# An emission planner's TensorE clock: a constant is added to each product's modelled time

## The chip, the cores and the metric

The program runs on one core of a Trainium2 chip. The time is that of the whole program on the device, in microseconds (us), taken as the median of several runs; less is better. A profiled execution gives the trace of every instruction. Engines are named as the profile does: PE is TensorE (PEld its weight loads), DVE is VectorE, ACT is ScalarE, POOL is GpSimd, SP is the sync engine, which issues the weight DMAs.

## What is computed

Two transformer blocks over 256 tokens of 1024 features, in float32. Cut to what matters:

```python
def reference(x, p, ...):
    x = first_block(x, p, ...)          # layer 0 and layer 1
    return second_block(x, p_2, ...)    # the third layer

def first_block(x, p, ...):
    for i in range(2):
        h = rms_norm(x, g[0])
        m = neighborhood_attention(h, ...) if i == 0 else diff_attention(h, ...)
        x = x + rms_norm(m, g[1])
        x = x + rms_norm(conv_glu_ffn(rms_norm(x, g[2]), ...), g[3])   # width 2816
        x = x + sigmoid(rms_norm(x, g[4]) @ ple_w_gate[i]) * (p[i] @ ple_w_proj[i])
    return x

def second_block(x, p, ...):
    h = x + 0.5 * swiglu(...)                       # width 2816
    u = rms_norm(h) @ w_in                          # the mixer
    o_hg = rms_norm(hgrn2_chunkwise(...)) * silu(hg)    # gated linear recurrence, 4 heads
    o_mla = causal_block_attention(...)             # latent attention, 4 heads
    h = h + concat([o_hg, o_mla]) @ w_out
    h = h + 0.5 * swiglu(...)
    h = h + sigmoid(rms_norm(h) @ w_ple_gate) * (p @ w_ple_proj)
    return rms_norm(h)
```

## The kernel before

Weights arrive in pieces of 128 x 1024 numbers, in the order in which they are used: SP issues the DMA into `raw` (5 buffers), ACT copies it to `hi` (rounded to the type fp32r), DVE subtracts the two into `lo` (9 buffers of each). Activations are split in the same manner (`xh` and `xl`, or a pair of `gx`). A float32 product is then three fp32r products on PE, high by high, high by low and low by high (`mm3`). Streams of such products are nearly all that PE does: with 256 columns where the result is feature-major (`s_chunk`), with 512 where it is token-major (`MStage`, which works on the two halves of 128 tokens apart).

Between these products stand short groups of plain fp32 products: scores of the attentions (`qk`), transposes of probabilities (`cst,e`), probabilities by values (`v,pts`), turns of a head's output (`flip,on`), transposes of the normed input of the next stage (`cst,xs`), and the steps of the recurrence (`qp,kp`, then `hvt,at` and `hvt,qr`, then transposes `cst,hgt` of the normed output). In the recurrence the heads go in two groups of two pairs; a group is done in one PSUM bank `pss`.

Each engine carries out its instructions in the order of its queue. That order is fixed as the program is built. A small model, `Model`, keeps a clock for each engine while the program is emitted: `Engine.call` passes an instruction on (which is why all of the profile's rows show one line, L237) and moves the clocks by the duration that `Engine.cost` gives. `MStage` and `s_chunk` emit the products one by one and call `q()` after each: this emits every other step whose operands are ready by the model's PE clock (plus H = 0.6 us), and calls `fill(t)`, which emits the `hi` or `lo` of a later weight where the model has ACT or DVE idle at that time. `get` and `get_any` choose among the PSUM banks in the same way. So a modelled duration sets where an instruction stands in its queue, and nothing else; on the chip it takes the time that it takes. `take()` emits a weight's parts at the latest before the product that needs them.

The line of the change, in `Engine.cost`, gives a product's duration from its columns n:

```python
            n = free(ins[1])
            dur = n / 2400 * (2 if name == "transpose" else 1 if ins[1].dtype == F32R and n >= 256 else 4)
```

Of the kernel before, what the change touches and what calls it, by code (L numbers as in the profile page):

```python
# [28 lines left out]

# columns of the packed per-feature vectors  # L30
COLS = {}
# [13 lines left out]
NCOL = _col_layout()  # L45
# columns of the shape-only constants
C_ID, C_CM, C_FX, C_NA, C_LV = 0, 128, 384, 385, 385 + 384
# [46 lines left out]
def _spairs(wa, wb):  # L94
    """Chunks of one 128-column block of wa and the same one of wb."""
    k, n = wa.shape
    w = np.stack([wa, wb]).reshape(2, k // 128, 128, n // 128, 128)
    return w.transpose(3, 2, 0, 1, 4).reshape(n // 128, 128, -1)
# [61 lines left out]
class Model:  # L160
    """Engine clocks in us as the program is emitted: they only choose the order of emission."""

# [64 lines left out]
class Engine:  # L227
    """Passes instructions on and keeps the model's clocks."""

# [20 lines left out]
    def cost(self, name, outs, ins, func):  # L250
        free = lambda ap: math.prod(ap.shape[1:])
        n = max(free(ap) for ap in outs + ins)
        ps = any(ap.space == PSUM for ap in outs + ins)
        if name == "dma_start":
            size = outs[0].shape[0] * n * 4 / 330e3
            return 1.04 if self.k == "POOL" else 0.06, [o for o in outs if o.space == SBUF], ins, size
        if self.k == "PE":
            n = free(ins[1])
            dur = n / 2400 * (2 if name == "transpose" else 1 if ins[1].dtype == F32R and n >= 256 else 4)
        elif self.k == "ACT":  # L260
            small = sum(1 for ap in ins if free(ap) == 1 and n > 1) + (len(outs) > 1)
            dur = ((61 if ps else 112) + n) / 1200 + 0.093 * small
            s = self.m.SETS.get(func)
            if s and s != self.m.set:
                self.m.set = s
                dur += 1.28
        elif self.k == "DVE":
            rate = 1.0
            if name == "reciprocal":
                rate = 7.0  # L270
            elif name == "tensor_tensor_scan":
                rate = 1.0
            elif name in ("tensor_scalar", "tensor_copy") and not ps:
                rate = 0.5
            scalar = name in ("tensor_scalar", "scalar_tensor_tensor") and any(
                free(ap) == 1 and ap.space == SBUF for ap in ins[1:]
            )
            dur = (66 + n * rate) / 960 + 0.061 * scalar
        else:
            dur = dict(tensor_tensor=0.3 + 0.164 * n, tensor_scalar=0.262).get(name, 0.02 + n * 0.85e-3)  # L280
        return dur, outs, ins
# [3 lines left out]
def body(ctx: ExitStack, tc: tile.TileContext, A: dict, out: bass.AP, dbg=None):  # L285
# [37 lines left out]
    def get(*tags):  # L323
        """In a step: waits for banks and for the operands of a product."""
        at = cur[0][1] + TO_PE - SP
        while True:
            free = [sorted(banks[t])[tags.count(t) - 1:] for t in tags]
            if all(free):
                at = max([at] + [f[0] + TO_PE - SP for f in free])
                if at <= M.now + 1e-6:  # L330
                    return [claim(t) for t in tags]
                yield (at,)
            else:
                yield (M.now + 0.3,)

    def get_any(*tags):
        """In a step: waits for a bank of any of these kinds."""
        at = cur[0][1] + TO_PE - SP
# [11 lines left out]
    def get_now(*tags):  # L350
        """In the products: waits for banks."""
        until(lambda: all(len(banks[t]) >= tags.count(t) for t in tags))
        return [claim(t) for t in tags]

    def put(*tags):
        """The last reader has been emitted."""
        for t in tags:
            banks[t].append(M.fin)

    def slot(n, shape, dt=F32, name="g"):  # L360
        """One of the 4 KB slots that the stages share."""
        return M.tile(big, 1, shape, dt, f"g{n}", name)
# [14 lines left out]

    # ---- the order of emission: products in quanta; everything else in steps between them, each
    # when the model has its operands ready ----
    fg, cur = [], [None]  # L380
# [49 lines left out]

# [1 line left out]
    subs = []  # L432
# [38 lines left out]
    def fill(t):  # L471
        """Parts of later weights, on engines that the model has idle."""
        while not W["hold"]:
            i = W["next"]
            if lows and M.clk["DVE"] <= t:
                prep_lo()
            elif i in raws and raws[i][1] <= t and i - W["freed"] < NS and len(lows) < 2 and M.clk["ACT"] <= t:
                prep()
            else:
                return  # L480
# [12 lines left out]

# [1 line left out]
    def split(hi, lo, src):  # L495
# [7 lines left out]
    def mm3(o, s, m, first, last):  # L503
        """o += s.T @ m for operands in (hi, lo) parts."""
        pe.matmul(o, s[0], m[0], start=first, stop=False)
# [6 lines left out]
    class Rows(list):  # L512
        """Feature-major operand; a half of it is ready once its writers are emitted."""

# [7 lines left out]
    class MStage:  # L522
        """Token-major acc[half][column block] = lhs.T @ W, contraction outermost."""

# [80 lines left out]
    def s_chunk(p, xt):  # L605
        """p[:, 256 b : 256 b + 256] = (W block b).T @ xt, for a pair of blocks."""
        for b in range(2):
# [8 lines left out]

# [1 line left out]
    def rstd(ss, n, dim):  # L618
# [6 lines left out]
    def rstd2(ss):  # L625
        """From two partial mean squares."""
        ms = sm.tile([128, 1], F32, tag="ms2", name="ms2")
# [30 lines left out]
    def norm_T(h, ss, gi, xt, pair=None, slow=True):  # L658
        """xt[:, half h] = (x rows * rstd * gain).T"""
        rs = rstd2(ss)  # L660
# [48 lines left out]
    def epi_post(h, acc, ok, gp, gi, xt, pair=None):  # L709
        """x += rms_norm(acc) * gp, then the next norm's transposed rows."""  # L710
        ss = sm.tile([128, 2], F32, tag="ss", name="ss")
# [27 lines left out]
    def epi_add(h, acc, ok, scale, gi, xt, pair=None):  # L739
        """x += scale * acc, then the next norm's transposed rows."""  # L740
        ss = sm.tile([128, 2], F32, tag="ss", name="ss")
# [11 lines left out]
    def epi_gate(h, acc, ok, pp, after, warm=False):  # L753
        """x += sigmoid(acc) * pp."""
        cut = [(0, 512), (512, 768), (768, 1024)] if len(acc) == 3 else [(0, 512), (512, 1024)]
# [32 lines left out]

# [1 line left out]
    def ffn_in(i, xt):  # L790
# [32 lines left out]

# [1 line left out]
    def ple_load(i, free=lambda: True):  # L825
        """The transposed embedding in parts, ahead of its product."""
        pt = w2([128, 512], "pt")
# [46 lines left out]

# [1 line left out]
    def na_bias(bm):  # L876
# [120 lines left out]

# [1 line left out]
    def t5_table():  # L999
# [109 lines left out]

# [1 line left out]
    def rope_tables():  # L1111
# [25 lines left out]
    def lower_bound():  # L1137
        """Columns: lb (4 heads), 1 - lb (4 heads)."""
        c0 = COLS["lb"]
# [23 lines left out]
    def mixer(xt):  # L1163
# [20 lines left out]
        ready = [None] * 8  # L1184
        # latent queries and keys, token-major; recurrent gates
        cq = slot(13, [128, 2, 448], name="cq")
# [57 lines left out]
        for h in range(2):  # L1244
            for m in (mc, mg):
                for c in range(4):
                    m.mm(c, h)
        # recurrent queries and gates, feature-major
        def gates(hd):
# [13 lines left out]
        for hd in range(HB):  # L1263
            gates(hd)
        # up-projections
        until(lambda: st["ct"] is not None)
# [43 lines left out]

    def hgrn(g, HQ, KP, QP, FT, TT, HV, HG, AT, ATC, AX_, masks, ready, st):
        """Two heads' scores by doubling: spans of length n meet over QP = q * (decay from the span's start) and
        KP = k * (decay to the span's end); every factor is a product of gates."""
        hs, cs_ = slice(2 * g, 2 * g + 2), slice(4 * g, 4 * g + 4)
# [21 lines left out]
        n = 1  # L1336
        while n < 128:
# [8 lines left out]
            else:  # L1346
                act.activation(at[0:64, :, 64:128], bank[0:64, 0:256].rearrange("p (a t) -> p a t", a=4), AF.Copy)
            # spans of length 2 n
            nb = 512 // (2 * n)
# [105 lines left out]

# [1 line left out]
    for nm in ("na", "da"):  # L1457
# [43 lines left out]
    def first(xt):  # L1501
        """Both halves of the first norm, together with the first weights."""
        ss = [sm.tile([128, 2], F32, tag="ss", name="ss") for _ in range(2)]
# [121 lines left out]
```

## Time and profile before

| | |
|---|---|
| median of 3 runs | 1234.1 us (1233.93 to 1235.17) |
| the profiled execution, its span | 1236.9 us (an execution of its own: no other time of it is listed) |
| PE busy | 1210.5 us of the span, 98% |
| DVE busy, ACT busy | 793.3 us, 702.3 us |
| mean granted clock of PE | 0.991 |
| DMA | 214.52 MB, 173 GB/s on average |

How to read it: PE is at work nearly all of the time, so what a change can win or lose lies in the stretches where PE waits, and in those after them where its granted clock is at the lower of its two levels. The span is 2.8 us over the median; a difference in us that is read from the trace is carried over to the median as it is.

### The profile page before, as it was taken

How to read it: one execution, taken by the hardware profiler on the slowest of the kernel's cores; microseconds unless marked ns; L12 is line 12 of the kernel's file. 1: busy time of each engine (PE TensorE's matmuls, PEld its weight loads, DVE VectorE, ACT ScalarE, POOL GpSimd, SP SyncE). 2: the span in 40 equal slices, each digit the busy share in tenths (PEclk: the TensorE clock that was granted, in tenths of full speed). 3: DMA queues.
4: the chain of work that ended last, by engine and by line, in shares of the span. 5: the costliest groups of instructions: out<-in, count | busy, mean ns of one | idle time of the engine just before them, and what ended most of it. 6: DMA issues, size and time to landing. Idle time of an engine off the chain costs nothing.

```text
span 1236.9 us, 21626 instructions
## 1 busy us (share of the span) xinstructions
PE 1210.5 (98%) x8550; PEld 1097.7 (89%) x8550; DVE 793.3 (64%) x1461; ACT 702.3 (57%) x1273; POOL 50.0 (4%) x89
## 2 busy tenths in 40 slices
PE   8999999999989998999999999999999999999997
PEld 6998899998869877999988799998898789999886
DVE  6866776664666876886645765554566676555445
ACT  6556865553766566765545754443565576444344
POOL 0000100000100212000000000000000010000001
PEclk8999999999999998999999999999999999999999
DMA  8835365565265224575563276555443266555630
GB/s 277 255 136 196 123 226 188 186 204 192 99 221 188 85 92 143 181 257 194 186 209 135 90 267 204 186 179 194 137 162 121 78 204 226 184 186 182 210 121 34
DMA packets 61798, 214.52 MB, mean 173 GB/s; under 512 B 7001, under 2 KB 9817, under 8 KB 61697
## 3 DMA queue, kind: packets, MB, share of 16 engines
q1 hardware_dynamic: 61696, 213.15, 51.6%
q8 instruction: 67, 1.10, 0.4%
q14 instruction: 35, 0.28, 0.1%
HBM read 211.01 MB, written 1.06 MB: 171 GB/s over the span
## 4 chain that ended last, share of the span: by engine, by line
PE 75%; issue 18%; DVE 2%; ACT 2%; POOL 1%; DMA 1%; POOLq 0%; ACTq 0%
PE psa L237 39%; PE pss L237 18%; PE pst L237 18%; POOL rs L237 1%; DVE lo L237 1%; POOL ms L237 1%; ACT junk L237 0%; DMA raw<-in_fi 0%; DMA x<-in_x 0%; ACT xh L237 0%; DVE x L237 0%; DVE xl L237 0%; ACT e L237 0%; DVE e L237 0%; DVE sct L237 0%
## 5 line engine op out<-in xcount | busy, mean ns | idle before, releaser
L237 DVE TENSOR_TENSOR lo<-raw,hi 128x1024 fp32r<-128x1024 f32 (+1 forms) x390 | 471.8, 1216 | 196.8 <-ACT hi L237 195.0
L237 ACT ACTIVATE hi<-raw 128x1024 fp32r<-128x1024 f32 (+1 forms) x390 | 405.9, 1051 | 241.1 <-PE psa L237 103.2
L237 PE MATMUL psa<-hi,gx 128*128 128x512 f32 (+1 forms) x1088 | 344.4, 391 | 2.6 <-ACT gx L237 2.3
L237 PEld LDWEIGHTS psa<-hi,gx 128*128 128x128 f32 x1088 | 204.5, 189 | 45.7 <-ACT gx L237 3.4
L237 PE MATMUL psa<-lo,gx 128*128 128x512 f32 (+1 forms) x544 | 211.2, 388 | 1.5 <-DVE lo L237 1.4
L237 PE MATMUL pst<-xh,hi 128*128 128x256 f32 x704 | 199.2, 283 | 0.0
L237 PE MATMUL pst<-xl,hi 128*128 128x256 f32 x704 | 199.2, 283 | 0.0
L237 PE MATMUL pst<-xh,lo 128*128 128x256 f32 x704 | 199.2, 283 | 0.0
L237 PE MATMUL pss<-xh,hi 128*128 128x256 f32 x672 | 190.5, 283 | 0.7 <-DVE xl L237 0.6
L237 PE MATMUL pss<-xl,hi 128*128 128x256 f32 x672 | 190.3, 283 | 0.0
L237 PE MATMUL pss<-xh,lo 128*128 128x256 f32 x672 | 190.2, 283 | 0.0
L237 PEld LDWEIGHTS pst<-xh,hi 128*128 128x128 f32 x704 | 135.2, 192 | 0.0
L237 PEld LDWEIGHTS pst<-xl,hi 128*128 128x128 f32 x704 | 135.2, 192 | 0.0
L237 PEld LDWEIGHTS pst<-xh,lo 128*128 128x128 f32 x704 | 135.2, 192 | 0.0
L237 PEld LDWEIGHTS pss<-xh,hi 128*128 128x128 f32 x672 | 129.0, 192 | 2.2 <-DVE xl L237 1.0
L237 PEld LDWEIGHTS pss<-xl,hi 128*128 128x128 f32 x672 | 129.0, 192 | 0.2 <-DVE xl L237 0.2
L237 PEld LDWEIGHTS pss<-xh,lo 128*128 128x128 f32 x672 | 129.0, 192 | 0.0
L237 PEld LDWEIGHTS psa<-lo,gx 128*128 128x128 f32 x544 | 102.7, 189 | 21.6 <-DVE lo L237 2.3
L237 PE MATMUL psa<-xh,hi 128*128 128x256 f32 x352 | 105.6, 300 | 1.0 <-ACT xh L237 1.0
L237 PE MATMUL psa<-xl,hi 128*128 128x256 f32 x352 | 100.7, 286 | 0.3
L237 PE MATMUL psa<-xh,lo 128*128 128x256 f32 x352 | 100.1, 284 | 0.0
L237 PEld LDWEIGHTS psa<-xh,hi 128*128 128x128 f32 x352 | 67.6, 192 | 6.8 <-issue 4.7
(239 smaller groups left out, 1441.4 us busy)
## 6 DMA issues: line engine op xcount, KB each, us to landing
raw<-in_fi SPq DMA_DIRECT2D x176, 512.0 KB, 4.6
raw<-in_fo SPq DMA_DIRECT2D x88, 512.0 KB, 3.8
raw<-in_pg SPq DMA_DIRECT2D x24, 512.0 KB, 4.1
raw<-in_na_qk SPq DMA_DIRECT2D x16, 512.0 KB, 5.2
raw<-in_da_qk SPq DMA_DIRECT2D x16, 512.0 KB, 5.6
raw<-in_na_v SPq DMA_DIRECT2D x8, 512.0 KB, 7.5
raw<-in_na_o SPq DMA_DIRECT2D x8, 512.0 KB, 3.6
raw<-in_da_v SPq DMA_DIRECT2D x8, 512.0 KB, 3.7
```

The costliest lines, as they stand in the source:

```text
L237: r = f(*a, **kw)
```

## The change

The duration of a product in the model gets a constant: 13.3 ns for one with fp32r operands, 2.5 ns for any other. An fp32r product of 256 columns goes from 0.1067 us to 0.1200 us, one of 512 from 0.2133 us to 0.2267 us. (An fp32r operand of fewer than 256 columns, which cost four times its columns before, now counts as 256.) The other lines of the diff only take out comments and are left out here.

```diff
         if self.k == "PE":
             n = free(ins[1])
-            dur = n / 2400 * (2 if name == "transpose" else 1 if ins[1].dtype == F32R and n >= 256 else 4)
+            if ins[1].dtype == F32R:
+                dur = max(n, 256) / 2400 + 0.0133
+            else:
+                dur = n / 2400 * (2 if name == "transpose" else 4) + 0.0025
```

The program has the same instructions after it, in another order. Three places:

**V of layer 1, on DVE.** `lo<-raw` is the low part of a weight piece; the pieces of V are, in order of use, raw_3823, then raw_3849 (before) or raw_3846 (after), then raw_3884. `sg`, `x` and `xs` belong to the last norm of layer 0's end, for the second half of the tokens, and `xl` is the split of its transposed result. Before:

```order
L237 TENSOR_TENSOR sg_4013<-sg_4013,pp_1631 128x512
L237 TENSOR_TENSOR x_86<-x_86,sg_4013 128x512
L237 TENSOR_TENSOR lo_3949<-raw_3823,hi_3948 128x1024
L237 TENSOR_SCALAR xs_4067<-x_86,rs2_4064 128x512
L237 TENSOR_TENSOR lo_3969<-raw_3849,hi_3968 128x1024
L237 SCALAR_TENSOR_TENSOR xl0_3748<-pss_4086,cols_88,xh0_3747 128x128
```

After:

```order
L237 TENSOR_TENSOR lo_3944<-raw_3823,hi_3943 128x1024
...
L237 TENSOR_TENSOR sg_4019<-sg_4019,pp_1631 128x512
L237 TENSOR_TENSOR x_86<-x_86,sg_4019 128x512
L237 TENSOR_TENSOR lo_3952<-raw_3846,hi_3951 128x1024
L237 TENSOR_SCALAR xs_4073<-x_86,rs2_4070 128x512
L237 TENSOR_TENSOR lo_3975<-raw_3884,hi_3974 128x1024
L237 SCALAR_TENSOR_TENSOR xl0_3776<-pss_4092,cols_88,xh0_3775 128x128
```

The low part of raw_3823 stood behind the second `x` and now stands twelve rows ahead of it (the rows left out are the eight `xl` of the first half, an `sg` and an `x`); each later one has moved up by one place, so that the one of raw_3884, which came behind the eight `xl` of this half, now stands ahead of them.

**The last two heads of layer 1's attention, on PE.** `v0, v1` by `pts` is the product of a head's values by its probabilities, into `pst`; it is normed, and `flip` turns the normed `on`. Before, pst_5503 is followed (the rows left out are six and three products of 512 columns):

```order
L237 MATMUL pst_5503<-v0_4037,pts_5506 128x128
L237 MATMUL pst_5503<-v1_4038,pts_5506 128x128
L237 MATMUL pst_5454<-flip_94,on_5508 128x128
...
L237 MATMUL pst_5546<-cst_87,e1_5403 128x128 x2
...
L237 MATMUL pst_5546<-v0_4037,pts_5549 128x128
L237 MATMUL pst_5546<-v1_4038,pts_5549 128x128
L237 MATMUL pst_5503<-flip_94,on_5551 128x128
L237 MATMUL psa_5261<-hi_5497,gx_4258 128x512
```

After, pst_5535:

```order
L237 MATMUL pst_5535<-v0_4045,pts_5538 128x128
L237 MATMUL pst_5535<-v1_4046,pts_5538 128x128
L237 MATMUL pst_5557<-cst_87,e1_5432 128x128 x2
L237 MATMUL psa_5282<-hi_5369,gx_4261 128x512
L237 MATMUL psa_5282<-lo_5370,gx_4261 128x512
L237 MATMUL psa_5282<-hi_5369,gx_4261 128x512
L237 MATMUL pst_5557<-v0_4045,pts_5560 128x128
L237 MATMUL pst_5557<-v1_4046,pts_5560 128x128
L237 MATMUL pst_5535<-flip_94,on_5583 128x128
L237 MATMUL psa_5281<-hi_5379,gx_4261 128x512
```

Between a head's `v,pts` and its `flip` stood nine products of 512 columns, another head's `flip`, transposes and values; now three products stand there, with the other head's transposes and values.

**The end of the recurrence in the last mixer, on PE and DVE.** `hvt` by `at` and `qr` ends the second group; `cst,hgt` transposes its normed output. On PE before (30 products of 512 columns stand between, all but one left out, and the first group's transposes):

```order
L237 MATMUL pss_10962<-hvt_10090,at_10096 128x128 x2
L237 MATMUL pss_10962<-hvt_10090,qr_10093 128x128
...
L237 MATMUL pss_10520<-cst_87,hgt_10091 128x128 x4
...
L237 MATMUL psa_11281<-hi_11285,gx_10756 128x512
L237 MATMUL pss_10962<-cst_87,hgt_10091 128x128 x4
L237 MATMUL psa_11239<-hi_11309,gx_11308 128x512
```

After (15 such products stand between, all but one left out):

```order
L237 MATMUL pss_11083<-hvt_10090,at_10096 128x128 x2
L237 MATMUL pss_11083<-hvt_10090,qr_10093 128x128
...
L237 MATMUL psa_11204<-hi_11160,gx_11276 128x512
L237 MATMUL pss_11083<-cst_87,hgt_10091 128x128 x4
L237 MATMUL psa_11203<-hi_11228,gx_11448 128x512
```

On DVE, `ms` is the mean square, from which POOL makes `rs`, and `hgt` is the norming. Before:

```order
L237 SCALAR_TENSOR_TENSOR gx_11308<-pss_10520,cols_88,gx_11308 128x256 x2
L237 TENSOR_SCALAR ms_11344<-ss4_11315 128x4
L237 TENSOR_TENSOR lo_11355<-raw_11111,hi_11354 128x1024
L237 SCALAR_TENSOR_TENSOR hgt_10091<-pss_10962,rs_11345,hgt_10091 128x128 x4
L237 TENSOR_TENSOR lo_11367<-raw_11192,hi_11366 128x1024
```

After:

```order
L237 TENSOR_TENSOR lo_11384<-raw_11244,hi_11383 128x1024
L237 TENSOR_TENSOR lo_11414<-raw_11344,hi_11413 128x1024
L237 TENSOR_SCALAR ms_11419<-ss4_11389 128x4
L237 TENSOR_TENSOR lo_11430<-raw_11366,hi_11429 128x1024
L237 SCALAR_TENSOR_TENSOR hgt_10091<-pss_11083,rs_11420,hgt_10091 128x128 x4
```

The second group has been moved later in the program (a latent attention's scores take its bank first), while the products that use its result stay where they were: fewer products lie between `hvt` and the transposes, and on DVE the `lo` ahead of `ms` is now one of which ACT makes the `hi` behind the sums of squares that `ms` reads.

## Rows read from the trace of the kernel before

**Rows 1.** The page: the span, and the busy time of each engine.

```profile
span 1236.9 us, 21626 instructions
...
PE 1210.5 (98%) x8550; PEld 1097.7 (89%) x8550; DVE 793.3 (64%) x1461; ACT 702.3 (57%) x1273; POOL 50.0 (4%) x89
```

**Rows 2.** Busy time and granted clock of one stretch, by windows (columns: us; PE, PEld, DVE, ACT, POOL busy; PEclk; DMA share; GB/s).

```profile
358.00:361.00 3.00, 3.00 (x8) 2.33 (x8) 3.00 (x4) 0.86 (x1) 0.00 (x0) 0.50 0.72 213
```

**Rows 3.** Timeline of TensorE, 60 us (columns: start, us, engine, line, operation, tiles, shapes, count).

```profile
60.48 0.36 PE L237 MATMUL psa<-xh,hi 128*128 128x256 f32 x1
60.68 0.28 PE L237 MATMUL psa<-xl,hi 128*128 128x256 f32 x1
60.80 0.28 PE L237 MATMUL psa<-xh,lo 128*128 128x256 f32 x1
```

**Rows 4.** Timeline of TensorE, layer 1, products that make V.

```profile
347.25 0.39 PE L237 MATMUL psa<-hi,xh 128*128 128x512 f32 x1
...
349.29 0.39 PE L237 MATMUL psa<-hi,xh 128*128 128x512 f32 x1
350.07 0.50 PE L237 MATMUL psa<-lo,xh 128*128 128x512 f32 x1 [0.39 <-DVE lo L237]
...
352.54 0.50 PE L237 MATMUL psa<-lo,xh 128*128 128x512 f32 x1 [0.81 <-DVE lo L237]
...
353.11 0.27 PE L237 MATMUL pss<-cst,xs 128*128 128x128 f32 x1
...
354.69 0.40 PE L237 MATMUL psa<-hi,xh 128*128 128x512 f32 x1
357.60 0.75 PE L237 MATMUL psa<-lo,xh 128*128 128x512 f32 x1 [2.51 <-DVE lo L237]
...
361.13 0.39 PE L237 MATMUL psa<-hi,xh 128*128 128x512 f32 x1
```

**Rows 5.** Timeline of DVE in the same stretch.

```profile
351.27 1.22 DVE L237 TENSOR_TENSOR lo<-raw,hi 128x1024 fp32r<-128x1024 f32 x1
...
356.33 5.76 DVE L237 TENSOR_TENSOR lo<-raw,hi 128x1024 fp32r<-128x1024 f32 x5
```

**Rows 6.** Timeline of TensorE, end of layer 1's attention.

```profile
450.74 0.50 PE L237 MATMUL psa<-lo,gx 128*128 128x512 f32 x1 [1.37 <-DVE lo L237]
...
463.56 0.60 PE L237 MATMUL pst<-v,pts 128*128 128x128 f32 x4
...
467.25 0.49 PE L237 MATMUL pst<-flip,on 128*128 128x128 f32 x2
...
473.31 0.50 PE L237 MATMUL psa<-hi,gx 128*128 128x512 f32 x1 [1.86 <-ACT gx L237]
...
477.29 0.39 PE L237 MATMUL psa<-lo,gx 128*128 128x512 f32 x1
```

**Rows 7.** Timeline of POOL in that stretch.

```profile
453.95 0.55 POOL L237 TENSOR_TENSOR rs<-ms,nhalf 128x1 f32<-128x1 f32 x1 [6.19 <-DVE ms L237]
...
465.41 1.40 POOL L237 TENSOR_TENSOR rs<-ms,nhalf 128x1 f32<-128x1 f32 x1 [2.31 <-DVE ms L237]
```

**Rows 8.** Timeline of TensorE, end of the last mixer.

```profile
989.67 0.60 PE L237 MATMUL pss<-hvt,at 128*128 128x128 f32 x4
...
998.32 0.60 PE L237 MATMUL pss<-cst,hgt 128*128 128x128 f32 x4
```

**Rows 9.** Timeline of ACT there.

```profile
992.19 0.22 ACT L237 ACTIVATION_READ_ACCUMULATOR junk<-pss 128x1 f32 x1
...
993.74 3.90 ACT L237 ACTIVATE hi<-raw 128x1024 fp32r<-128x1024 f32 x4
998.95 0.48 ACT L237 ACTIVATE gx<-pss,cols 128x256 fp32r<-128x256 f32 x1 [1.31 <-PE pss L237]
```

**Rows 10.** Timeline of DVE there.

```profile
994.28 0.16 DVE L237 TENSOR_SCALAR ms<-ss 128x4 f32<-128x4 f32 x1
...
995.97 1.12 DVE L237 SCALAR_TENSOR_TENSOR hgt<-pss,rs,hgt 128x128 f32<-128x128 f32 x4
```

## The prediction, written before the kernel was run

> **What bounds the kernel now.** The page comes first: PE is busy for 1210.5 of 1236.9 us [rows 1]. The weights, the splits and the steps between products are on engines that are busy for 793 us at most, so the products' own time is a floor that an order can't move; what is open is the waiting between them and the clock behind a wait.
>
> The timeline of PE then gives the price of a product that waits for nothing. Two fp32r products of 256 columns start 0.12 us apart (60.68 to 60.80) [rows 3]. Ten of 512 columns start from 347.25 to 349.29, nine steps of 0.2267 us [rows 4]. Less columns by 2.4 GHz (0.1067 and 0.2133), both leave 0.0133 us. The model of before is short by that for every product, so its PE clock runs ahead of the chip's own pace; the changed one agrees with these rows. This says only that the planner's clock is truer, not that its order is better: it emits a step where the model has its operands ready plus H, and what was late on the chip may have been so by other durations (ACT, DVE, POOL, DMA), which stay as they were.
>
> The third view is the timeline around PE's waits, to see who came last. Three places matter.
>
> *V of layer 1.* PE waits for a `lo` of DVE three times: 0.39 us at 350.07, 0.81 at 352.54, 2.51 at 357.60 [rows 4]. From start to start, less 0.227, they cost 0.55 (349.29 to 350.07), 0.98 (the idle 0.81 and 0.17 of emptying the array, as at the other two) and 2.68 us (354.69 to 357.60). Behind the last one the granted clock is 0.50, the lower of the two levels, 1.2 GHz [rows 2], and eight products take 3.53 us to 361.13, where 1.82 would do: 1.71 us more. In all 5.9 us.
>
> *End of layer 1's attention.* 1.37 us for a `lo` at 450.74, and 1.86 us for `gx` at 473.31; behind the second the ten products to 477.29 take 3.98 us where 2.27 would do, 1.71 us more [rows 6]. In all 4.9 us.
>
> *End of the recurrence.* Nothing is lost there before: from `hvt` at 989.67 to the transposes at 998.32 PE has products to do [rows 8].
>
> **The change part by part.** The instructions are the same, so only places in queues are costed. Each sum is made in the profiled execution, whose span is 2.8 us above the median; I carry the difference over to 1234.1 us.
>
> *V of layer 1.* Each `lo` is one place earlier in DVE's queue: that of the piece which PE waited for at 350.07 is made long before, and the one made in its place serves the next piece. The `lo` that ended the wait at 352.54 started at 351.27 [rows 5]; it now serves a piece that PE wants only six products (1.36 us) later. So the first two waits go (1.53 us), and PE comes to the transposes of `xs` at 351.6 and not at 353.11. What is late next is the first `lo` behind the eight `xl`. Before, from the transposes to the product that had waited for such a `lo` it took 4.49 us (353.11 to 357.60) [rows 4, 5], and PE had 1.81 us of work in between. After, it has six products more: 4.49 - 1.81 - 1.36 = 1.3 us of waiting, and I add 0.3 for transposes that may meet `xs` before it is made. With no drop of the clock behind so short a wait: 5.9 - 1.6 = 4.3 us won. With a drop 2.6; with neither the 0.3 nor a drop 4.6.
>
> *End of layer 1's attention.* The parts of the weights are emitted well ahead, so the 1.37 us go. The last `gx` now has six products ahead of its use and fewer `hi` ahead of it on ACT, so the 1.86 us go. But between the values of a head (`v,pts`) and its `flip` nine products have become three. Before, the pair took 3.69 us from 463.56 to 467.25, hardly waiting [rows 6]: sums of squares on ACT, `ms`, `rs` on POOL, `on` on DVE. The work that PE now has in that time is about 1.75 us (three products 0.68, the other head's transposes and values 0.7, the switches). That gives 1.9 us of waiting; two `lo` now stand ahead of `ms`, so up to 2.8; I take 2.2. POOL's `rs` is part of that chain: it took 0.55 us at 453.95 and 1.40 at 465.41 [rows 7], and I count the long one, since a `lo` stands behind `ms` here too. By the Trainium skill (SBUF — State Buffer, section on the two separate sides) DVE and POOL share a port pair, which the one that is first holds for its whole instruction, so that POOL waits out a `lo`; by the short `rs` the wait would be 0.85 us less and the total by as much lower. By that rule the long one is right, and the two durations agree with it. Net 2.7 us won (4.9 - 2.2); if the clock drops behind the new wait, 1.0; at the long end of the wait with a drop, 0.4; at the short end without, 3.0 and, with the short `rs`, 3.8.
>
> *End of the recurrence.* The transposes of the second group come 15 products behind `hvt` and not 30. Let `hvt` start at T. Before, the sums of squares ended at 992.41, T + 2.7 [rows 8, 9]. Behind them ACT now makes the `hi` (0.98 us, four in 3.90 [rows 9]) whose `lo` (1.22 [rows 5]) DVE has ahead of `ms`: `ms` starts at T + 5.0. From `ms` to `hgt` it took 1.69 us (994.28 to 995.97) and `hgt` 1.12 [rows 10], so `hgt` is done at T + 7.8, and the transposes start at T + 8.0. PE gets there at T + 1.26 (the group itself) + 15 x 0.227 + 0.1 = T + 4.8: 3.2 us of waiting where there was none. Then the next product wants `gx`: ACT started it 0.63 us after the transposes, for 0.48 us [rows 8, 9], against 0.36 us of transposes: 0.8 us more. Together 4.0. Queued behind the waiting transposes are all the products of the output projection, and nothing else can go on PE. If ACT had that `hi` made before the sums of squares, it would be 2.3 us less. The wait is longer than the 2.51 us that were followed by the lower clock, so I add 1.7: 5.7 us lost; bounds 1.7 and 6.
>
> *Groups of fp32 products between fp32r ones.* By the order there are nine more of them (120 before, 129 after), since steps are no longer emitted in one batch. Behind such a group the first step is 0.20 us where 0.12 is due (60.48 to 60.68) [rows 3], 0.08 more; ahead of it I take as much. Nine by 0.16 is 1.4, by three times 0.08 is 2.2; I take 1.7 us lost.
>
> *The feed-forward parts and the rest.* There `hi` and `lo` are made tens of products ahead before and after, and PE waits for none of them: nothing, give or take 1 us for small waits that come or go.
>
> Sum: -4.3 - 2.7 + 5.7 + 1.7 = +0.4 us. Within the halves of this sum that I trust least (whether the clock drops) that is no change: 1234.4 us.
>
> **The rivals.**
>
> *The gains stay and the losses don't come (faster).* If ACT's `hi` is made in time, the wait at the recurrence is 1.7 us and no drop follows it, and the sum is -4.3 - 2.7 + 1.7 + 1.7 = -3.6, 1230.5 us; with the short `rs` 1229.6. For it: the parts of the weights are emitted earlier nearly everywhere in the order, so ACT may be less pressed. Against it: ACT's queue has the `hi` behind the sums.
>
> *Both new waits drop the clock (slower).* At the attention's end the new wait (2.2) is nearer to the 1.86 us that were followed by the lower clock than to any that wasn't [rows 6]. Then its gain is 1.0 and the sum +2.1; with the wait at its long end (0.6 more) and V's shorter gain of 2.6 (1.7 more) it is +4.4: 1236.2 to 1238.5 us. It decides from a wait of about 2 us at the `flip` on.
>
> *The order changes and the time doesn't.* PE is fed in all the long stretches, and if V's waits only move to the pieces behind (its gain 2.6 at least) while recurrence and attention give their losses back, the sum stays within 1 us: this lies with my forecast. By the Trainium skill (TensorE: Matmul & The Clock Gate, on the back-to-back gap) an isolated product takes its columns and 2.5 ns, so that the new constant would be 10.8 ns too long and the planner late to the other side; the 13.3 ns of the rows at 60.68 and 347.25 speak against that, and I give it nothing.
>
> **How the numbers follow.** Less than 0.2%, 2.5 us, can't be told from no change here. The forecast with its own range of 1231.7 to 1236.5 has 0.38; the faster rival, with what may be won beyond it by small waits, 0.32, down to 1227 us; the slower one, with new small waits, 0.30, up to 1241. To leave out no more than 2 in 10, one of each side: 1228.5 to 1239.5 us. Faster 0.32, same 0.38, slower 0.30.
>
> **What would show it.** In the profile after: V of layer 1 with one wait for `lo` of 1 to 1.6 us, near 353 to 356, and full clock behind it; the end of layer 1's attention with a wait of 2 us for `on` ahead of a `flip`, and none for `lo`; near 990 to 1000 a wait of 3 us for `hgt` ahead of `cst,hgt`, with products at the lower clock behind it. Wrong would be: V with its 2.5 us wait still there (the planner's places then don't decide it, a DMA or POOL does); no wait at the recurrence (the `hi` came earlier than the queue says); or new waits in the feed-forward parts, where I expect none.

## The result, and the profile after

The changed kernel takes 1250.8 us (median of 4 runs, 1247.16 to 1252.3) against 1234.63 us before (4 runs): the ratio is 1.0115, with a 95% interval of 1.0094 to 1.0137. The ratio goes by the means, 1250.3 against 1236.0: it is slower by 14 us (the medians differ by 16), and outside the range that was given. The profiled execution has a span of 1248.9 us against 1236.9 [rows 1], a time of its own of 1250.92 us, and a mean granted clock of 0.987 against 0.991. In the executions whose time and span are both listed the span is some 2 us below the time, so the one profiled before, with 1236.9, took about 1239 us, some 3 us over the mean; that is why the two profiles lie only 12.0 us apart.

All 7326 fp32r products stand in the same order in both, so the start of the same product in both traces tells where the time went (us; products numbered from 0; the differences are computed from the two timelines of PE):

```text
product   before    after     difference   what lies between this row and the one above
26        20.02     19.72     -0.30        start
562       120.20    124.29    +4.09        layer 0: attention and its output projection
653       140.00    145.82    +5.82        handover to layer 0's feed-forward part
1914      320.00    325.83    +5.83        feed-forward part
1991      340.01    346.89    +6.88        its end and the gate
2047      360.29    363.04    +2.75        V of layer 1
2602      480.04    482.48    +2.44        layer 1: rest of the attention
2710      500.05    504.46    +4.41        handover to layer 1's feed-forward part
3869      660.17    664.58    +4.41        feed-forward part
4167      720.09    725.50    +5.41        gate, handover to the third layer
5820      1000.15   1005.24   +5.09        feed-forward part, mixer but for its end
5899      1020.05   1031.20   +11.15       end of the mixer, handover
7318      1228.02   1239.17   +11.15       feed-forward part, gate
```

V of layer 1 wins 4.1 us and the end of the mixer loses 6.1, both as forecast. What was not forecast is 4.4 us in layer 0's attention, 1.7 and 2.0 us at the two handovers, 1.0 us at each of the two gates, and that the rest of layer 1's attention wins next to nothing (0.3).

PE's waits by what ended them, the longest groups (columns: what waited, for what; us in total, times, the longest):

```profile
PE pss L237 <- DVE xs L237: 7.2, 5, 1.9
PE pss L237 <- DVE hgt L237: 3.3, 1, 3.3
PE psa L237 <- ACT xh L237: 2.8, 2, 1.4
PE pss L237 <- ACT qk L237: 2.1, 3, 0.9
PE psa L237 <- ACT gx L237: 2.1, 4, 0.6
...
PE psa L237 <- DVE lo L237: 1.3, 1, 1.3
PE pst L237 <- DVE ms L237: 1.3, 1, 1.3
PE psa L237 <- ACT qk L237: 1.2, 1, 1.2
```

In layer 1's V one wait is left of three, 1.35 us idle at 363.04 (from start to start, less 0.227, it is 1.51), where [rows 4] have 0.39, 0.81 and 2.51. The timeline of PE after:

```profile
361.30 0.39 PE L237 MATMUL psa<-hi,xh 128*128 128x512 f32 x1
363.04 0.50 PE L237 MATMUL psa<-lo,xh 128*128 128x512 f32 x1 [1.35 <-DVE lo L237]
```

Three windows of the profile after, each behind a wait (columns as in [rows 2]; the granted clock is the number behind POOL's `(x0)`), say that full speed went on behind this wait, and that the lower level, 1.2 GHz, came behind the waits at the ends of the mixer and of layer 1's attention:

```profile
1013.00:1017.00 4.00, 4.00 (x10) 3.11 (x10) 2.53 (x5) 0.99 (x2) 0.00 (x0) 0.50 0.27 100
473.50:475.30 1.80, 1.80 (x5) 1.42 (x5) 0.91 (x1) 0.69 (x2) 0.00 (x0) 0.50 0.97 310
363.00:366.00 3.00, 2.96 (x13) 2.47 (x14) 3.00 (x3) 0.36 (x1) 0.00 (x0) 1.00 0.57 201
```

The end of the mixer, PE after, which answers to [rows 8]: 3.26 us for `hgt`, then 0.56 for `gx`, then products of 0.43 us from start to start:

```profile
1011.38 0.66 PE L237 MATMUL pss<-cst,hgt 128*128 128x128 f32 x4 [3.26 <-DVE hgt L237]
1012.60 0.80 PE L237 MATMUL psa<-hi,gx 128*128 128x512 f32 x1 [0.56 <-ACT gx L237]
1013.19 0.63 PE L237 MATMUL psa<-lo,gx 128*128 128x512 f32 x1
1013.62 1.06 PE L237 MATMUL psa<-hi,gx 128*128 128x512 f32 x2
```

DVE there, which answers to [rows 10]:

```profile
1006.86 1.23 DVE L237 TENSOR_TENSOR lo<-raw,hi 128x1024 fp32r<-128x1024 f32 x1 [1.56 <-ACT hi L237]
1008.01 0.16 DVE L237 TENSOR_SCALAR ms<-ss 128x4 f32<-128x4 f32 x1
...
1010.20 1.12 DVE L237 SCALAR_TENSOR_TENSOR hgt<-pss,rs,hgt 128x128 f32<-128x128 f32 x4 [0.90 <-POOL rs L237]
```

And ACT there ([rows 9]): the sums of squares end at 1005.88, two `hi` follow:

```profile
1005.66 0.22 ACT L237 ACTIVATION_READ_ACCUMULATOR junk<-pss 128x1 f32 x1
1005.75 2.02 ACT L237 ACTIVATE hi<-raw 128x1024 fp32r<-128x1024 f32 x2
```

The first of these two `hi` ends near 1006.7; the `lo` that DVE has ahead of `ms` starts at 1006.86 and holds `ms` until 1008.01. This is the chain of the prediction, with two sizes off that nearly cancel: `ms` starts 4.8 us behind `hvt` (1003.20) and not 5.0, and `hgt` comes 2.19 us behind `ms` and not 1.69, because POOL's `rs` in between took 1.91 us where it had taken 1.01 before:

```profile
1008.25 1.91 POOL L237 TENSOR_TENSOR rs<-ms,nhalf 128x4 f32<-128x4 f32 x1 [16.33 <-DVE ms L237]
```

The end of layer 1's attention, PE after ([rows 6]): between `v,pts` at 467.98 and its `flip` at 471.74 PE waits 0.17 and 1.34 us, then 0.46 for `gx`, and the clock falls.

```profile
467.98 0.61 PE L237 MATMUL pst<-v,pts 128*128 128x128 f32 x4
...
469.69 0.71 PE L237 MATMUL pst<-v,pts 128*128 128x128 f32 x4 [0.17 <-ACT pts L237]
471.74 0.49 PE L237 MATMUL pst<-flip,on 128*128 128x128 f32 x2 [1.34 <-DVE ms L237]
472.69 0.80 PE L237 MATMUL psa<-hi,gx 128*128 128x512 f32 x1 [0.46 <-ACT gx L237]
```

At the handovers to the feed-forward parts, which no row ahead of the prediction shows, ACT after has a `hi` between `xs` and `xh`:

```profile
134.42 0.72 ACT L237 ACTIVATE xs<-x,rs 128x512 f32<-128x512 f32 x1
135.04 1.04 ACT L237 ACTIVATE hi<-raw 128x1024 fp32r<-128x1024 f32 x1
135.99 1.06 ACT L237 ACTIVATE pp<-psa 128x512 f32<-128x512 f32 x2
136.95 0.47 ACT L237 ACTIVATE xh<-pss,cols 128x256 fp32r<-128x256 f32 x1
```

Before, in the same place:

```profile
130.33 0.72 ACT L237 ACTIVATE xs<-x,rs 128x512 f32<-128x512 f32 x1
130.96 1.06 ACT L237 ACTIVATE pp<-psa 128x512 f32<-128x512 f32 x2
131.91 0.47 ACT L237 ACTIVATE xh<-pss,cols 128x256 fp32r<-128x256 f32 x1
```

The `hi` takes 0.95 us of ACT's queue, and `xh` comes as much later behind `xs` (2.53 us from start to start, where it was 1.58). PE waits for it, after:

```profile
134.96 0.33 PE L237 MATMUL pss<-cst,xs 128*128 128x128 f32 x1 [0.99 <-DVE xs L237]
...
137.47 0.39 PE L237 MATMUL psa<-xh,hi 128*128 128x256 f32 x1 [1.42 <-ACT xh L237]
...
138.31 0.42 PE L237 MATMUL psa<-xh,lo 128*128 128x256 f32 x1
138.53 0.42 PE L237 MATMUL psa<-xh,hi 128*128 128x256 f32 x1
```

and before:

```profile
130.87 0.33 PE L237 MATMUL pss<-cst,xs 128*128 128x128 f32 x1 [1.02 <-DVE xs L237]
...
132.44 0.38 PE L237 MATMUL psa<-xh,hi 128*128 128x256 f32 x1 [0.47 <-ACT xh L237]
...
133.30 0.29 PE L237 MATMUL psa<-xh,hi 128*128 128x256 f32 x1
133.42 0.31 PE L237 MATMUL psa<-xl,hi 128*128 128x256 f32 x1
```

It waits 1.42 us for `xh` and not 0.47, and the products behind it are 0.22 us apart after (138.31 to 138.53), the lower level, where two of before are 0.12 apart (133.30 to 133.42). The handover at 490 us has like waits (0.93 and 1.42); behind it the lower level holds for 6.2 us, from 490.17 to 496.40, where before it held for 3.5, from 487.29 to 490.80.

In layer 0's attention PE waits for scores' operands (`qk`), 0.48 and 0.71 us after, where it waited for none before:

```profile
45.58 1.09 PE L237 MATMUL pss<-qk 64*64 64x128 f32 x16 [0.48 <-ACT qk L237]
...
53.32 0.87 PE L237 MATMUL pss<-qk 64*64 64x128 f32 x12 [0.71 <-ACT qk L237]
```

ACT made its half of the first of these `qk` just ahead of it, released by DVE's half of the same copy out of PSUM:

```profile
45.14 0.38 ACT L237 ACTIVATE qk<-psa 128x256 f32<-128x256 f32 x1 [3.04 <-DVE qk L237]
```

DVE's half is the late one. After:

```profile
43.81 0.96 DVE L237 TENSOR_TENSOR nabias<-rpbraw,namask 128x128 f32<-128x128 f32 x3
44.70 0.41 DVE L237 TENSOR_SCALAR qk<-psa 128x256 f32<-128x256 f32 x1
```

Before, and the scores on PE, which wait for nothing:

```profile
41.52 0.96 DVE L237 TENSOR_TENSOR nabias<-rpbraw,namask 128x128 f32<-128x128 f32 x3
42.41 0.41 DVE L237 TENSOR_SCALAR qk<-psa 128x256 f32<-128x256 f32 x1
```

```profile
44.61 1.09 PE L237 MATMUL pss<-qk 64*64 64x128 f32 x16
```

On PE these scores stand behind the same 168 fp32r products in both kernels. On DVE 17 `lo` and 12 `nabias` stand ahead of the first `qk` after, 16 and 9 before: one `lo` (1.21 us) and three `nabias` (0.96) more, and `qk` starts 2.29 us later.

And in the output projection a product waits for a PSUM bank that `qk` frees; that `qk` too is late on DVE (102.91), behind a `lo` (100.77) and the scaling of `e` (102.12):

```profile
103.80 0.50 PE L237 MATMUL psa<-hi,gx 128*128 128x512 f32 x1 [1.18 <-ACT qk L237]
```

At the two gates (341 and 694 us) PE waits 0.5 us for `gx` of ACT and 0.2 for `gx` of DVE, where it waited for nothing before. No run takes these by themselves; the kernel with three places undone, below, still has them.

### The profile page after: what moved, and what is told of

The parts are those of the page before. It is cut to its first block, busy times and chain, and to the rows that moved or that the text cites. A ratio compares the mean times of both kernels' runs of the same rounds, so it can differ in the third digit from the quotient of the medians.

```text
span 1248.9 us, 21731 instructions
## 1 busy us (share of the span) xinstructions
PE 1214.8 (97%) x8550; PEld 1100.4 (88%) x8550; DVE 797.9 (64%) x1461; ACT 697.9 (56%) x1273; POOL 49.2 (4%) x89
## 4 chain that ended last, share of the span: by engine, by line
PE 65%; DVE 2%; ACT 1%; POOL 1%; issue 0%; POOLq 0%; DVEq 0%; ACTq 0%
PE psa L237 30%; PE pss L237 17%; PE pst L237 17%; DVE lo L237 1%; POOL rs L237 0%; ACT junk L237 0%; DVE gx L237 0%; ACT xh L237 0%; DVE sct L237 0%; ACT hi L237 0%; ACT gx L237 0%; DVE e L237 0%; DVE on L237 0%; DVE x L237 0%; DVE sg L237 0%
## 5 line engine op out<-in xcount | busy, mean ns | idle before, releaser
L237 PE MATMUL psa<-hi,gx 128*128 128x512 f32 (+1 forms) x1088 | 348.5, 394 | 3.8 <-ACT gx L237 2.1
L237 PEld LDWEIGHTS psa<-xh,hi 128*128 128x128 f32 x352 | 69.3, 197 | 10.1 <-issue 5.2
```

Of the source, the lines that this page charges most:

```text
L237: r = f(*a, **kw)
```

## The experiments

Two theories stood at first. **Places**: the loss is a sum of a few places at which the order tips over, each with its own wait. **Margin**: the short clock of before gave every step a margin, which goes as the constant grows, so the loss grows with it. Four kernels with other constants tell them apart.

```diff
-                dur = max(n, 256) / 2400 + 0.0133
+                dur = max(n, 256) / 2400 + 0.0067      # half; 0.0133, 0, 0.02 in the others
-                dur = n / 2400 * (2 if name == "transpose" else 4) + 0.0025
+                dur = n / 2400 * (2 if name == "transpose" else 4) + 0.00125   # 0, 0.0025, 0.0025
```

**Half of the constants.** 

> Half of each constant (6.7 ns for an fp32r product, 1.25 ns for any other). Theory P (places): the 12 us are the sum of a few places where the order tips over: a hi ahead of xh on ACT at both feed-forward handovers, the recurrence's transposes, scores in layer 0, less the gain at V of layer 1. By its order this kernel has no hi between xs and xh at the handovers, 27 products of work (6.6 us) between hvt and the transposes where the change has 15 (3.4), and V's low parts one place ahead as in the change: P expects V's 4 us gained and none of the losses but one or two, 1228 to 1236 us. Theory M (margin): the short clock of before gave each step some products' worth of margin, and the loss grows with the constant: about halfway, 1240 to 1244 us.

Measured: 1239.48 us (10 runs, 1234.74 to 1241.88), ratio 1.0024 (1.0006 to 1.0042), a little under what Margin gives and over what Places gave: neither range holds it. In its trace V wins 3.8 us (the product 2047 starts at 357.79), no `hi` stands at the handovers, the mixer's end has no wait; but at 443.83 PE waits 2.51 us for a `lo` of layer 1's output projection, which is new, and in layer 0's attention 1.4 us for a `qk`. The profiled execution is the fastest of the ten, so it doesn't show where the mean loses 3 us.

**Only the fp32r products.** 

> The 13.3 ns for fp32r products alone, nothing for the others. P: by its order one of the two handovers has the hi ahead of xh (layer 0), the other has not, the recurrence has 4.8 us of products between (the change 3.4, before 7.2), the last flip only 0.7 us after its values: 1243 to 1249 us. M: the constant of the fp32r products is nearly all of the margin, so as the change, 1249 to 1252 us.

Measured: 1257.79 us (4 runs, 1256.69 to 1259.4), ratio 1.0182 (1.0156 to 1.0207). Slower than with both constants, which Margin can't give, and slower than Places had it by what it had counted: the last `flip` of layer 1's attention, 0.7 us of products behind its values, waits much longer than the order seemed to say. PE there (timeline of the kernel with the fp32r constant alone):

```profile
470.06 0.50 PE L237 MATMUL psa<-hi,gx 128*128 128x512 f32 x1 [0.52 <-ACT gx L237]
...
477.73 0.49 PE L237 MATMUL pst<-flip,on 128*128 128x128 f32 x2 [3.78 <-DVE on L237]
480.27 0.79 PE L237 MATMUL psa<-hi,gx 128*128 128x512 f32 x1 [2.05 <-ACT gx L237]
```

3.78 us for `on`, which DVE started at 477.33 behind two `mg`, a `lo` and two `x`, and 2.05 for `gx`; by the start of the same products this stretch (460 to 480 us) costs 7.3 us more than before.

**Only the others.** 

> The 2.5 ns for all other products alone, fp32r products as before. P: by its order the handovers, the recurrence and V's low parts stand as before, some attention steps move: 1232 to 1238 us. M: no margin lost: 1234 to 1236 us. Not a test between the two but of which half of the edit acts.

Measured: 1233.67 us (10 runs, 1231.71 to 1236.2), ratio 0.9980 (0.9964 to 0.9996): the 2.5 ns by themselves win a little. In the profiled execution it lies in layer 1's attention (product 2602 starts 5.8 us earlier than before, 2.8 of which are lost again by 960 us). The loss is from the fp32r constant, and the two halves of the edit don't add: without the 2.5 ns the change is 0.67%, some 8 us, slower still.

**Half as much again.** 

> A constant of 20 ns for fp32r products in place of 13.3. P: both handovers have the hi ahead of xh as in the change, the recurrence has 4.8 us of products between rather than 3.4, the flips at the end of layer 1's attention 2.2 us and more: 1243 to 1250 us, no more than the change. M: the loss grows by half again: 1256 to 1260 us.

Measured: 1243.51 us (4 runs, 1242.43 to 1244.45), ratio 1.0065 (1.0040 to 1.0090). A longer constant, a shorter time than the change's: Margin falls. Places had its lower end right. In its trace the transposes at the mixer's end don't wait for `hgt`, and that stretch (products 5820 to 5899) costs 2.0 us and not 6.1; the waits at the handovers are those of the change.

The next four undo or do one place alone. The change was not run again beside them: each is set against it by the two ratios to the kernel before. The first two start from the change. In the first the constants are variables of the model, which are 0 while the mixer is emitted:

```diff
+    M.c1, M.c2 = 0.0, 0.0
     lhs = mixer(xt)
...
+    M.c1, M.c2 = 0.0133, 0.0025
     G = ffn_in(3, xt)
```

> The change, with the old durations (no constant) while the last mixer is emitted, up to its feed-forward part. Order: the same as the change up to the mixer; there 7.2 us of products between hvt and the last transposes as before. Theory P (places: each waits for itself): the 3.4 and 0.7 us of waiting and the half clock behind them go, and the products from 1000 us on come 5 to 6 us earlier: 1244 to 1247 us. Theory D (the waiting is given back: the weights and the next norm are late as well, so that a wait saved at one place is paid at the next): 1249 to 1252 us.

Measured: 1244.48 us (4 runs, 1243.48 to 1244.83), ratio 1.0072 (1.0046 to 1.0098), that is 0.43% or 5.3 us below the change's ratio. The waits of 3.26 and 0.56 us are gone. The loss there is a place, and it isn't given back.

The second holds the stream of weight parts for one step at the handovers:

```diff
         xs = scaled(h, rs)
+        if pair and h == 1:
+            W["hold"] = 1
         yield
+        W["hold"] = 0
```

> The change, with the stream of weight parts held while the second half's xs waits for its transposes at the handovers to the two feed-forward parts (and the same at the others of that kind), so that no hi stands between xs and xh on ACT. P: the wait for xh goes from 1.42 to 0.47 us at both (137 and 490 us), and with less waiting the lower clock behind them need not come, 1.5 us each: 1246 to 1249 us. D: the hi is late later and the time stays, 1249 to 1252 us.

Measured: 1243.59 us (4 runs, 1242.28 to 1245.42), ratio 1.0065 (1.0041 to 1.0088), 0.50% or 6.2 us below the change's; the expectation's upper end of the gain was 5. PE's wait for `xh` at the first handover, and at the second (timeline of this kernel):

```profile
134.37 0.39 PE L237 MATMUL psa<-xh,hi 128*128 128x256 f32 x1 [0.48 <-ACT xh L237]
```

```profile
484.12 0.39 PE L237 MATMUL psa<-xh,hi 128*128 128x256 f32 x1 [0.47 <-ACT xh L237]
```

0.48 and 0.47 us, as before the change. By the start of the same products the two handovers give 1.7 and 2.7 us. The other 2.2 us of these two profiled executions up to 60 us lie where the two programs have the same order, so they are chance; 1.3 more come at the end of layer 1's attention, where the clock doesn't fall in this execution.

**V alone, from the kernel before.**

```diff
+        if i == 0:
+            M.c1, M.c2 = 0.0067, 0.00125
         MStage(xt2, D, 8, lambda h, acc, ok: epi_gate(h, acc, ok, pp, after, i == 1), cut=i == 1).run(*GL[i])
...
         V = v_stage(xt, 8)
+        M.c1, M.c2 = 0.0, 0.0
```

> Before, with half of the constants (6.7 and 1.25 ns) only from layer 0's gate to the end of V of layer 1. Order: as before everywhere but there, where the low parts stand one place ahead as in the change. P: the three waits of 0.55, 0.98 and 2.68 us become one of 1.5 to 2.0 and the half clock behind it goes: 3.4 to 4.3 us less than before, a ratio of 0.9965 to 0.9972. D: the time comes back at the end of layer 1's attention: within 1 us of before.

Measured: 1234.25 us (12 runs, 1231.91 to 1236.48), ratio 0.9985 (0.9972 to 0.9998): 1.9 us faster, half of what was expected. The trace shows a reason (timeline of PE in this kernel):

```profile
356.54 0.50 PE L238 MATMUL psa<-lo,xh 128*128 128x512 f32 x1 [1.86 <-DVE lo L238]
...
358.33 0.63 PE L238 MATMUL psa<-lo,xh 128*128 128x512 f32 x1
...
360.89 0.49 PE L238 MATMUL psa<-lo,xh 128*128 128x512 f32 x1
```

One wait of 1.86 us is left, and 1.3 us behind it the products are 0.43 us apart until 360.89: the clock falls here, as it didn't behind the change's 1.35. At product 2047 this kernel is 3.7 us ahead of before, at product 2151, behind the slow stretch, 2.4. That is this execution: in the kernel with half of the constants throughout PE waited as long there (1.85 us at 357.79) and the products behind stayed at full speed.

**V and the 2.5 ns.** The same edit with `M.c1, M.c2 = 0.0, 0.0025` on both sides of the stretch.

> As the kernel with 2.5 ns for all products that aren't fp32r (fp32r without a constant), with half of the constants only from layer 0's gate to the end of V of layer 1. Order: V as in the change, layer 1's attention with at least 3.5 us of products between values and flip, no hi ahead of xh at the handovers, the mixer's end as before. P: the two gains add: 3.4 to 4.3 us at V and 2 to 3 at the end of layer 1's attention, 1227 to 1230 us, ratio 0.994 to 0.996. D: 1231 to 1235 us.

Measured: 1230.43 us (12 runs, 1227.4 to 1233.91), ratio 0.9955 (0.9942 to 0.9969). This version is faster than the kernel before by 5.6 us and than the change by 20; V's gain alone was 1.9 and that of the 2.5 ns 2.5, so within the intervals the two add.

What was left was layer 0's attention, and whether the places add up. From the change, with the model's constants at 0 until layer 0's attention is emitted:

```diff
         lhs = layer0_attn(xt, bm) if i == 0 else layer1_attn(xt)
+        if i == 0:
+            M.c1, M.c2 = 0.0133, 0.0025
```

> The change, with the old durations (no constant) from the start to the last step of layer 0's attention that is emitted with its products; the constants from its output projection on. Order: the hi ahead of xh at both handovers, layer 1 and the mixer as in the change. Theory P (places): the waits of the change for scores and probabilities (0.64 at 45.6, 0.87 at 53.3, 0.42 at 55.6 us), for xh at 36.2 (0.61) and for a bank behind qk at 103.8 (1.34) go, 3.9 us: 1246 to 1248 us. Theory S (layer 0's loss isn't the waits in its attention but the DMA that is busier there, so it stays whatever the order): 1249 to 1252 us.

Measured: 1246.02 us (5 runs, 1243.74 to 1248.72), ratio 1.0079 (1.0052 to 1.0106), 0.36% or 4.4 us below the change's, with an uncertainty nearly as large (the two intervals overlap); the trace decides. At product 544, in the output projection, it is 3.9 us ahead of the change, and the waits at 45, 53, 55 and 103 us are gone; on DVE the first `qk` has 16 `lo` and 9 `nabias` ahead of it again. So they were a matter of order; the DMA engines are about as busy there in all three (a share of the window from 20 to 60 us of 0.89 after, 0.86 before, 0.85 here).

**All three.** The edits of the mixer, the handovers and layer 0's attention together.

> The change with all three undone: layer 0's attention and the mixer emitted by the old durations, and the weight parts held at the handovers. If the places add up, the change's 1250.8 less 6.3 (mixer alone), 7.2 (handovers alone) and 3 to 4 (layer 0's attention): 1233 to 1235 us, that is the time of before, the gain at V of layer 1 being paid for by the turn at the end of layer 1's attention and the nine extra groups. If the losses overlap (one clock drop counted twice), 1236 to 1240 us.

Measured: 1237.35 us (10 runs, 1234.64 to 1238.12), ratio 1.0008 (0.9991 to 1.0024): no difference from before that can be told. Alone the three are worth 5.3, 6.2 and 4.4 us, 15.9; together 1.07% or 13.2 us. Of the change's 14 us nearly all is in these three; that the sum is over the whole by 2.7 us is within the intervals of the three ratios, some 3 us each. Between the two expectations it doesn't decide: 1237.35 us lies in the range for losses that overlap, but the kernel before took 1235.56 beside it, and the difference of 0.08% is nearer to places that add up.

## Why the prediction was wrong

**V of layer 1** was right: 4.3 us forecast, 4.1 measured by the start of the same products, with the one wait at the place and of the size forecast (1.3 us; 1.35 idle) and full clock behind it. Six other kernels here have the same wait (about 1.4 us), and full clock behind it too.

**The end of the recurrence** was right, up to two small sizes that nearly cancel: 5.7 us forecast, 6.1 measured; waits of 3.2 and 0.8 us forecast, 3.26 and 0.56 idle measured, and the lower clock behind them. The chain over the `hi` that ACT makes behind the sums of squares is the one that the rows after show, and the kernel with the old clock in the mixer takes it away.

**The end of layer 1's attention** was mis-sized. The waits for `lo` went and one ahead of a `flip` came, 1.34 us and not 2.2. The chain from values to `flip` took 3.76 us, as the prediction had it (3.69), and POOL's `rs` in it 1.40, the long one that it counted; but its 1.75 us of work for PE left out the head's own values (0.45 us, 467.98 to 468.43). To the 1.34 came 0.39, 0.17 and 0.46 us of other waits, and the clock fell as in the slower rival, for a shorter stretch (to 475.69, 3.0 us). From product 2151, behind V, to 2602 the change is level with before (0.05 us ahead), which holds that gain, a new wait of 0.94 us at 386.92 for `qk`, and the extra groups. The 2.7 us are not there.

**The nine extra groups**, 1.7 us, can't be read apart from the waits that they stand among; no run took them alone.

**The step that failed** is "the feed-forward parts and the rest: nothing, give or take 1 us". By the start of the same products the rest cost 10.1 us: 4.4 in layer 0's attention, 1.7 and 2.0 at the handovers, 2.1 at the gates. The step reasoned from the distance between a part's making and its use, and took earlier to be harmless. But a part that is made earlier takes its time of ACT or DVE at that earlier place. At both handovers a `hi` takes 0.95 us of ACT ahead of `xh`, on a chain that PE waits for. At the second, the change falls behind by 1.0 us from product 2602 to 2616, for the `hi` itself, and by 1.0 more to product 2643, where the lower clock holds longer; the kernel that holds the parts there has the losses of both handovers back. In layer 0's attention, of which the prediction didn't speak at all, a `lo` and three `nabias` more stand ahead of the first `qk` on DVE, while the scores that need it stand where they stood on PE. The order of ACT's queue at the handovers, and DVE's in layer 0's attention, would have shown both, as PE's and DVE's did in the three places that were looked at; PE was watched at the places where it waited before, and not at those where it didn't yet.

The rival that ended on the slower side had the right sign by the wrong way: its mechanism, the clock behind the `flip`, came true and cost little.

What stays open is why the planner puts these steps there: that the model's ACT and DVE seem idle for longer by a slower PE clock, so that `fill` finds room for a `hi` ahead of `xh` or a `lo` ahead of `qk`, is argued from the code and was not tried by itself. The 2.1 us at the gates were not undone either.

## What to carry to other kernels

A planner's durations are not measurements to be made truer one at a time: the order that they give is good or bad at a few places where a step tips over, and the time is not a smooth function of a constant (0, 6.7, 13.3 and 20 ns for an fp32r product: ratios of 1, 1.0024, 1.0115 and 1.0065). So compare the orders on every engine, and above all at places where PE doesn't wait yet but the chain behind it is short: handovers between stages, copies out of PSUM, norms. And where a new order gains at one place and loses at others, apply it to that place alone: here half of the constants at V alone, with 2.5 ns for the other products, won 5.6 us where the whole change lost 14.

## What was not expected of the hardware

The length of the waits just ahead doesn't settle whether the clock falls behind them. In like places, waits of nearly the same length (us idle) were followed by full speed in one case and by the lower level in the other:

- First and second handover of the kernel before: full speed behind 1.02 and 0.47 (130.87 and 132.44), the lower level behind 0.94 and 0.48 (485.20 and 486.77).
- End of layer 1's attention: the lower level behind 1.34 and 0.46 after, full speed behind 1.64 and 0.46 in the kernel that holds the parts at the handovers (467.89 and 468.84).
- V of layer 1: full speed behind 1.85 with half of the constants; with V alone, behind 1.86, full speed for 1.3 us and then the lower level for 3; with V and the 2.5 ns, behind 1.86, the lower level at once.

So waits of 1 to 2 us cost up to 1.7 us more behind them (1.3 in V alone, from product 2047 to 2151; 1.7 behind the 1.86 of [rows 6]), or nothing. That is one reason to judge by several executions and not by the profiled one.
